# Order of the first pages, sixteen gate products moved ahead, and the chunk recurrence as a thread of its own

## The chip, the cores and the metric

The kernel runs on one core of one Trainium2 chip. The metric is the device time of one execution in microseconds; the time before is the median of three runs. Engines are named as in the profile: PE (matmul), PEld (its weight loads), DVE (vector), ACT (scalar), POOL (GpSimd) and SP, which here only issues DMAs. A name such as L707 is a line of the kernel before.

## What is computed

One layer of a hybrid backbone: two parallel head groups over one input projection, then a gated MLP with a 3x3 convolution on a grid. D_MODEL is 2048, there are 512 latent and 256 context tokens, D_FF is 5632, all in float32. The reference, cut:

```python
mx = jnp.split(s_c @ w_ada + b_ada, 6, axis=-1)            # s_c = silu(c); mc the same for the context
h_ctx = modulate(rms_norm(ctx, g_pre_mix), mc[0], mc[1])
h_lat = modulate(rms_norm(x, g_pre_mix), mx[0], mx[1])
u_lat = h_lat @ w_in                                       # 2048 columns: 1536 for pooling, 512 for the SSM
u_ctx_ssm = h_ctx @ w_in[:, POOL_WIDTH:]
for d in range(2):                                         # two directions of a diagonal complex recurrence
    lam, bb = s5_discretise(...)                           # h_t = lam * h_{t-1} + bb u_t
    hc = s5_scan(ctx_g, lam, bb, None, rev)
    hl = s5_scan(lat_g, lam, bb, h0_from(hc), rev)
    lat_dirs.append(s5_readout(hl, c_re, c_im))
# pooling: centred means over 2, 4, 8, 16 tokens minus the token, a 384x384 matmul per group
mix = concat([pool_out, gelu(y + d*u) * sigmoid(. @ w_glu)]) @ w_out
x = x + mx[2] * rms_norm(mix, g_post_mix)
z = modulate(rms_norm(x, g_pre_ffn), mx[3], mx[4]) @ w_up
f = (val * silu(gate)) @ w_down                            # val, gate: halves of the 3x3 convolution of z
x = x + mx[5] * rms_norm(f, g_post_ffn)
```

## The kernel before

Every matmul on a weight is made of three: a weight page of 128x1024 is loaded on SP's queue (`raw`, L60), rounded by ACT to `whi` (L77), and DVE forms the rest, `wlo` = raw - whi (L78). PE then multiplies high by high, high by low and low by high (L176 to L178). `raw`, `whi` and `wlo` have two buffers each, and one page is made ahead. Each engine does its instructions in the order of the program.

The kernel goes through these stages.

*First pages.* Twelve pages of x and the context come in (`x_page`, L409), ACT squares them, and PE sums the squares over partitions into `ssl` and `ssc`. Among them `ada_round` R (L436) loads a 1 MB page of the modulation weights (`adak`, three buffers) and multiplies the condition with it; round n // 3 follows every third page. A table (`at`, `pre`) hangs other work behind given rounds: `rstd_x` behind round 4, then rows and columns of the modulation (`ada_row`, `ada_cols`), the tiles of h (L472 to L493), and pieces of the first projection (`u_piece`). `discretise1` to `discretise4` compute the powers of lam on POOL, with two sines on ACT (L321, L322); the second and third are called at page 8.

*First projection.* The columns of u for the SSM, of the latent tokens (`ul`) and the context (`uc`), go round by round with the rest of the ada rounds. POOL builds matrices `mi` (`mi_build`, L557 to L559) from the powers, and PE transposes them to `mt` (`mt_half`, L577): `mi` k behind round 13 + 3k, its halves behind 17 + 3k and 18 + 3k.

*Latent projection.* Twelve blocks of two pages (`u_block`, tile `ub`) give the pooling columns; a page is 24 matmuls. After each, `bg.tick` steps background threads (`Threads`, L90): generators that emit a little work and yield its DVE cost and a lag in pages. They are asked in the order of their priorities. `front` (0) stores u to DRAM, reads it back transposed as `UT` (SP, L658), multiplies it with `mt` into `bp` (L674), does the chunk recurrence on `B` (54 pairs of a product L691 and a sum L692 on DVE), and, once all blocks are out, goes on to the SSM's output (`SN`, `R`, E by matmuls `eb`, y). `pool_block` (1) forms the windows' means (`ps`, L854) and p (L865 to L872) from a block that ACT has evicted to `up` (L839). `gemv` (3) forms the other modulation vectors: 96 products of half a row block of `ada_n` (`gv`, 512 KB, two buffers) with the condition's row, summed by DVE (L924), in the order (vector c, block n, half).

*Pooling matmuls, output projection* (`pool_group`, `wout_block`), with the SSM output and the rest of `gemv` as threads among them.

*Turn to the FFN.* `norm_pair` (L1057) adds the first sub-layer to x, normalises, and forms h for the FFN: `macc` scaled rows, transposes to `h2p`, and `hf` (L1109, ACT L1106) with the scale and shift in `acol`. Those come from the last products: `bg.finish(gv_t)` (L1089) emits all that are left. Then come the up and down projections of the FFN.

## Time and profile before

| | before |
|---|---|
| median of three runs | 2239.28 us (2239.27 to 2248.13) |
| the profiled execution | 2241.74 us, its span 2240.0 us |
| PE busy in the span | 2098.5 us (94%) |
| DVE busy | 1543.1 us (69%) |
| ACT busy | 691.3 us (31%) |
| POOL busy | 285.3 us (13%) |
| DMA moved | 313.43 MB, a mean of 140 GB/s |

The shares are means over stages with different limits; the stages are read one by one from the table of windows in the section below. "Granted clock" is TensorE's clock as a share of the full one, as the profile records it.

### The profile page before, as it was taken

What the parts mean: (1) busy time and instruction counts of PE and PEld (TensorE: products, weight loads), DVE (VectorE), ACT (ScalarE), POOL (GpSimd) and SP (SyncE); (2) the same over time, 40 slices, a digit from 0 to 9 for tenths busy, and PEclk for the clock granted to TensorE, in tenths of its full rate; (3) what the DMA queues carried; (4) which work ended last, traced back from release to release, by engine and by line L of the source; (5) the groups of instructions that cost most, each with busy time, mean ns of one, the idle gap of its engine ahead of it and who ended that gap; (6) DMA issues with size and microseconds to landing.
All of it is one profiled execution on the core that took longest, in us unless ns stands there. A gap on an engine that the chain in (4) does not pass through costs nothing.

```text
span 2240.0 us, 24576 instructions
## 1 busy us (share of the span) xinstructions
PE 2098.5 (94%) x9500; PEld 1653.2 (74%) x9500; DVE 1543.1 (69%) x2134; ACT 691.3 (31%) x977; POOL 285.3 (13%) x334
## 2 busy tenths in 40 slices
PE   6998889899992899999999999999999999999996
PEld 3577667666772888888888888888888888888885
DVE  2543887654676588867777777777767667667676
ACT  3344215553352533332222222222222222222224
POOL 7940000571023200000000000000000000000004
PEclk9899999999995999999999999999999999999998
DMA  7855125765774423333333333333322333323335
GB/s 307 319 196 188 57 79 180 223 179 170 253 252 154 177 95 97 126 132 114 111 123 113 131 124 114 111 123 113 112 88 94 94 94 94 94 94 94 94 94 188
DMA packets 92564, 313.43 MB, mean 140 GB/s; under 512 B 16288, under 2 KB 21152, under 8 KB 88352
## 3 DMA queue, kind: packets, MB, share of 16 engines
q1 hardware_dynamic: 89920, 304.99, 40.9%
q10 hardware_dynamic: 2528, 6.88, 0.9%
q8 instruction: 74, 1.21, 0.2%
q14 instruction: 42, 0.34, 0.0%
HBM read 301.38 MB, written 10.45 MB: 139 GB/s over the span
## 4 chain that ended last, share of the span: by engine, by line
PE 65%; DMA 5%; DVE 4%; ACT 2%; issue 1%; POOL 0%; DVEq 0%; ACTq 0%; SPq 0%; POOLq 0%
PE up L177 14%; PE up L176 14%; PE up L178 14%; PE dn L176 7%; PE dn L178 7%; PE dn L177 7%; DMA gv<-in_ada_n 3%; DVE scr L924 1%; DMA raw<-in_w_out 1%; DMA raw<-in_w_up 1%; DVE wlo L78 1%; ACT scr L1038 0%; PE uh L178 0%; PE uh L176 0%; PE uh L177 0%
## 5 line engine op out<-in xcount | busy, mean ns | idle before, releaser
L78 DVE TENSOR_TENSOR wlo<-raw,whi 128x1024 fp32r<-128x1024 f32 (+1 forms) x326 | 404.6, 1241 | 422.6 <-ACT whi L77 419.7
L77 ACT ACTIVATE whi<-raw 128x1024 fp32r<-128x1024 f32 (+1 forms) x326 | 340.4, 1046 | 720.6 <-PE dn L178 313.4
L1225 DVE SCALAR_TENSOR_TENSOR cv<-zp,wconv,cv 128x512 f32<-128x512 f32 x704 | 528.3, 750 | 18.8
L176 PE MATMUL up<-h,whi 128*128 128x512 f32 x1344 | 531.3, 395 | 0.0
L177 PE MATMUL up<-h,whi 128*128 128x512 f32 x1344 | 530.9, 395 | 0.0
L178 PE MATMUL up<-h,wlo 128*128 128x512 f32 x1344 | 530.6, 395 | 0.0
L177 PEld LDWEIGHTS up<-h,whi 128*128 128x128 f32 x1344 | 252.0, 187 | 61.5
L178 PEld LDWEIGHTS up<-h,wlo 128*128 128x128 f32 x1344 | 251.9, 187 | 61.6
L176 PEld LDWEIGHTS up<-h,whi 128*128 128x128 f32 x1344 | 251.9, 187 | 61.6
L176 PE MATMUL dn<-whi,g 128*128 128x512 f32 x672 | 265.6, 395 | 0.0
L178 PE MATMUL dn<-whi,g 128*128 128x512 f32 x672 | 265.6, 395 | 0.0
L177 PE MATMUL dn<-wlo,g 128*128 128x512 f32 x672 | 265.3, 395 | 0.0
L1040 POOL TENSOR_TENSOR facc<-facc,frow 128x512 f32<-128x512 f32 x11 | 15.4, 1429 | 1437.7 <-ACT scr L1038 1437.7
L924 DVE SCALAR_TENSOR_TENSOR scr<-gv,srow 128x1024 bf16<-128x1024 f32 x96 | 131.2, 1366 | 84.0 <-DMA gv<-in_ada_n 79.0
L1259 ACT ACTIVATE zp<-up 128x512 f32<-128x512 f32 x84 | 50.6, 602 | 378.3 <-PE up L178 373.6
L178 PEld LDWEIGHTS dn<-whi,g 128*128 128x128 f32 x672 | 126.0, 187 | 31.0
L176 PEld LDWEIGHTS dn<-whi,g 128*128 128x128 f32 x672 | 126.0, 188 | 30.6
L177 PEld LDWEIGHTS dn<-wlo,g 128*128 128x128 f32 x672 | 126.0, 187 | 30.5
L1273 DVE TENSOR_TENSOR facc<-facc,dn 128x512 f32<-128x512 f32 x144 | 92.1, 681 | 0.7 <-PE dn L178 0.7
L176 PE MATMUL ub<-hT,whi 128*128 128x512 f32 x192 | 80.3, 418 | 10.6 <-ACT whi L77 10.5
L178 PE MATMUL ub<-hT,wlo 128*128 128x512 f32 x192 | 79.9, 416 | 8.9 <-DVE wlo L78 8.9
L177 PE MATMUL wo<-wlo,mx 128*128 128x512 f32 x192 | 77.0, 401 | 3.9 <-DVE wlo L78 3.9
(272 smaller groups left out, 2487.6 us busy)
## 6 DMA issues: line engine op xcount, KB each, us to landing
raw<-in_w_up SPq DMA_DIRECT2D x176, 512.0 KB
gv<-in_ada_n SPq DMA_DIRECT2D x128, 512.0 KB
raw<-in_w_down SPq DMA_DIRECT2D x88, 512.0 KB
adak<-in_ada_k SPq DMA_DIRECT2D x32, 1024.0 KB
raw<-in_w_out SPq DMA_DIRECT2D x32, 512.0 KB
raw<-in_w_inp SPq DMA_DIRECT2D x24, 512.0 KB
xl<-in_xT SPq DMA_DIRECT2D x8, 512.0 KB
raw<-in_w_ssm SPq DMA_DIRECT2D x8, 512.0 KB
```

The lines of the kernel that those rows point to most:

```text
L77: nc.scalar.activation(hi[:, :n], raw[:, :n], AF.Copy)
L78: nc.vector.tensor_tensor(lo[:, :n], raw[:, :n], hi[:, :n].bitcast(F32), op=OP.subtract)
L176: PE.matmul(o, ahi, bhi, start=start, stop=False)
L177: PE.matmul(o, ahi, blo, start=False, stop=False)
L178: PE.matmul(o, alo, bhi, start=False, stop=stop)
L924: V.scalar_tensor_tensor(scr[:], tiles[x][:], 1.0, srow[:, hf * 1024:(hf + 1) * 1024], op0=OP.mult, op1=OP.mult, accum_out=gacc[:, hf, c, ...
L1040: eng.tensor_tensor(m, m, row[d // 2][:, d % 2, :], op=OP.mult)
L1225: V.scalar_tensor_tensor(a[:], zz, wcol, a[:], op0=OP.mult, op1=OP.add)
L1259: S.activation(zp[j][i % 2][:, 1:9, 1:65], o.rearrange("p (r c) -> p r c", r=8), AF.Copy)
L1273: V.tensor_tensor(f, f, os[t], op=OP.add)
```

## The change

1. *First pages.* An ada round follows every second page, six among the pages for four before. `rstd_x` hangs behind round 5, `discretise2` and `discretise3` (before at page 8) behind round 7, `discretise4` behind 8. `mi` k is built behind round 14 + 4k, its halves are transposed behind 20 + 4k and 21 + 4k.
2. *Gate products.* Eight pages of 1 MB, each both halves of one block of the first vector, are loaded behind rounds 32 to 39 into the buffers of `adak`; two products each behind rounds 35 to 42. `gemv` leaves these 16 out.
3. *Recurrence.* It is a thread `scan` of priority 2, added when the last `bp` is out: behind `pool_block`, ahead of `gemv`. `front` goes on when blocks and `scan` are done. The lags in `front` around the store, UT and `bp` are longer.

```diff
@@ the table of rounds
-        at(13 + 3 * k, lambda k=k: mis.update({k: mi_build(k, pg("mi"), ...)}))
+        at(14 + 4 * k, lambda k=k: mis.update({k: mi_build(k, pg("mi"), ...)}))
         for r in range(2):
-            at(13 + 4 + 3 * k + r, lambda k=k, r=r: mt_half(k, r))
-    at(4, rstd_x)
-    at(5, discretise4)
+            at(20 + 4 * k + r, lambda k=k, r=r: mt_half(k, r))
+    at(5, rstd_x)
+    at(7, discretise2)
+    at(7, discretise3)
+    at(8, discretise4)
+    gpair = {}
+
+    def gpair_load(nt):
+        gpair[nt] = p0.tile([128, 2, 1024], F32, name="adag", tag="adak", bufs=3)
+        nc.sync.dma_start(gpair[nt][:], A["ada_n"][0, nt].rearrange("a p n -> p a n"))
+
+    def gpair_dot(nt):
+        g = gpair.pop(nt)
+        for hf in range(2):
+            V.scalar_tensor_tensor(scr[:], g[:, hf], 1.0, srow[:, hf * 1024:(hf + 1) * 1024], op0=OP.mult,
+                                   op1=OP.mult, accum_out=gacc[:, hf, 0, nt:nt + 1])
+
+    NGP = 8
+    for nt in range(NGP):
+        at(32 + nt, lambda nt=nt: gpair_load(nt))
+        at(35 + nt, lambda nt=nt: gpair_dot(nt))
@@ the twelve pages
-        if n == 8:
-            discretise2()
-            discretise3()
-        if n % 3 == 2:
-            ada_round(n // 3)
-            for f in rounds.get(n // 3, []):
+        if n % 2 == 1:
+            ada_round(n // 2)
+            for f in rounds.get(n // 2, []):
                 f()
-    for R in range(4, max(rounds) + 1):
+    for R in range(6, max(rounds) + 1):
@@ front, and the recurrence taken out of it
+    def scan():
+        ...
+        for c0 in (0, 16):
+            yield cma(B[:, c0 + 1:c0 + 16:2], B[:, c0:c0 + 15:2], l4[:, 0], 8), 0
+        ...
     def front():
         mi_next(NMT)
-        yield 0.0, 0.4
+        yield 0.0, 1.2
         ...                                     # UT loads
-        yield 0.0, 0.4
+        yield 0.0, 1.6
         ...                                     # k >= NMT: mt_half, mi_next
-                    yield 0.0, 0.2
+                    yield 0.0, 0.4
         ...                                     # bp
-                yield 0.0, 0.2
-        for c0 in (0, 16):
-            yield cma(B[:, c0 + 1:c0 + 16:2], B[:, c0:c0 + 15:2], l4[:, 0], 8), 0
-        ...
+                yield 0.0, 1.6 if k == NMT else 0.3
+        sc_t = bg.add(scan(), 2)
 
         while not ub_done:
             yield 0.0, 1
+        while not sc_t[2]:
+            yield bg._step(sc_t), 0
@@ gemv
-        todo = [(c, n, hf) for c in range(3) for n in range(16) for hf in range(2)]
+        todo = [(c, n, hf) for c in range(3) for n in range(16) for hf in range(2)][2 * NGP:]
-            gv_state[0] = x + 1
+            gv_state[0] = 2 * NGP + x + 1
```

The order that this gives is shown at three places. In it a line of the changed kernel is about 20 higher than the same line of before (from L650 on; ahead of that it differs by 0 or 1).

ACT's queue among the last of the twelve pages, before. `sq` are the squares, `sm` the sines of discretise2, `adar` a copied row of the modulation, `rst` part of rstd_x:

```order
L420 ACTIVATE sq<-xc_301 128x1024
L321 ACTIVATE sm<-sm 128x32
L322 ACTIVATE sm<-sm 128x32
L420 ACTIVATE sq<-xl_357 128x1024
L420 ACTIVATE sq<-xl_363 128x1024
L420 ACTIVATE sq<-xc_369 128x1024
L450 ACTIVATE adar<-ada_254 128x512
L403 ACT_TABLE_LOAD
L403 ACTIVATE rst<-rv 128x512
```

And in the changed kernel:

```order
L451 ACTIVATE adar<-ada_247 128x512
L420 ACTIVATE sq<-xc_316 128x1024
L420 ACTIVATE sq<-xl_324 128x1024
L420 ACTIVATE sq<-xl_337 128x1024
L420 ACTIVATE sq<-xc_343 128x1024
L403 ACT_TABLE_LOAD
L403 ACTIVATE rst<-rv 128x512
L403 ACTIVATE rst<-rv 128x256
L451 ACTIVATE adar<-ada_329 128x512
L321 ACT_TABLE_LOAD
L321 ACTIVATE sm<-sm 128x32
```

The sines have moved behind `rst`, with a load of ACT's function table of their own, and the first copy of an ada row stands ahead of the last four squares.

DVE's queue in the latent projection, between the splits of two pages, before. `sct` and `B` are the recurrence, `ps` and `p` the pooling:

```order
L78 TENSOR_TENSOR wlo<-raw,whi 128x1024
L691 TENSOR_TENSOR sct<-B,lp_86 128x512
L692 TENSOR_TENSOR B<-B,sct 128x8x64
L691 TENSOR_TENSOR sct<-B,lp_86 128x512
L692 TENSOR_TENSOR B<-B,sct 128x8x64
L854 TENSOR_TENSOR ps_1996<-up 128x527
L854 TENSOR_TENSOR ps_1998<-ps_1996 128x525
L854 TENSOR_TENSOR ps_2000<-ps_1998 128x521
L865 SCALAR_TENSOR_TENSOR p_1904<-ps_2000,up 128x512
```

And in the changed kernel:

```order
L78 TENSOR_TENSOR wlo<-raw,whi 128x1024
L875 TENSOR_TENSOR ps_2191<-up 128x527
L875 TENSOR_TENSOR ps_2193<-ps_2191 128x525
L886 SCALAR_TENSOR_TENSOR p_2201<-ps_2193,up 128x512
L888 TENSOR_TENSOR p_2201<-ps_2193,rcnt 128x2
L889 TENSOR_TENSOR p_2201<-p_2201,up 128x2
L892 TENSOR_TENSOR p_2201<-ps_2193,rcnt 128x1
L893 TENSOR_TENSOR p_2201<-p_2201,up 128x1
L666 TENSOR_TENSOR sct<-B,lp_86 128x64
L667 TENSOR_TENSOR B<-B,sct 128x64
```

The pooling of a block now stands ahead of the recurrence. The recurrence stands in pages 7 to 18 of the 24 before, and in pages 12 to 24 and the eight pooling-matmul pages behind them now. On PE, 36 matmuls of `ub` stand ahead of the first `bp` before, and 78 now.

DVE's queue in the turn to the FFN, before. `scr,gacc<-gv,srow` is a gate product, `macc` the rows that are normalised:

```order
L1083 TENSOR_SCALAR macc_3766<-xin,st_1359 128x1024
...
L924 SCALAR_TENSOR_TENSOR scr,gacc<-gv,srow 128x1024 x3
L1037 TENSOR_TENSOR macc_3767<-macc_3767,wq_4745 128x512
L1037 TENSOR_TENSOR macc_3768<-macc_3768,wq_4746 128x512
L924 SCALAR_TENSOR_TENSOR scr,gacc<-gv,srow 128x1024 x2
L1037 TENSOR_TENSOR macc_3767<-macc_3767,wq_4786 128x512
L1040 TENSOR_TENSOR macc_3767<-macc_3767,pio 128x512
L1037 TENSOR_TENSOR macc_3768<-macc_3768,wq_4787 128x512
L1040 TENSOR_TENSOR macc_3768<-macc_3768,pio 128x512
L924 SCALAR_TENSOR_TENSOR scr,gacc<-gv,srow 128x1024 x9
L934 TENSOR_TENSOR acol<-gacc 128x16
```

And in the changed kernel:

```order
L944 SCALAR_TENSOR_TENSOR scr,gacc<-gv,srow 128x1024 x2
L1057 TENSOR_TENSOR macc_3768<-macc_3768,wq_4762 128x512
L1057 TENSOR_TENSOR macc_3769<-macc_3769,wq_4763 128x512
L944 SCALAR_TENSOR_TENSOR scr,gacc<-gv,srow 128x1024
L954 TENSOR_TENSOR acol<-gacc 128x16
L955 TENSOR_TENSOR acol<-acol,colp 128x16
L959 TENSOR_SCALAR acol<-acol 128x16
L960 TENSOR_TENSOR acol<-acol,colp 128x16
L1057 TENSOR_TENSOR macc_3768<-macc_3768,wq_4800 128x512
L1060 TENSOR_TENSOR macc_3768<-macc_3768,pio 128x512
L1057 TENSOR_TENSOR macc_3769<-macc_3769,wq_4801 128x512
L1060 TENSOR_TENSOR macc_3769<-macc_3769,pio 128x512
```

Of 14 products that stood there 3 are left, and `acol` stands ahead of the last `macc` rows.

## Rows read from the trace of the kernel before

**Rows 1.** Windows by stage: stretch, its length, busy us of each engine (instructions), granted clock.

```profile
0.00:73.00 73.00, 49.98 (x214) 23.17 (x215) 24.13 (x49) 26.49 (x37) 57.79 (x156) 0.85 0.83 324
73.00:174.50 101.50, 101.50 (x635) 71.63 (x635) 47.69 (x48) 34.44 (x53) 64.85 (x52) 0.99 0.64 236
174.50:335.60 161.10, 129.81 (x579) 103.02 (x578) 113.88 (x203) 44.52 (x86) 9.18 (x6) 0.92 0.32 102
335.60:667.00 331.40, 313.44 (x1453) 238.58 (x1451) 217.98 (x311) 149.72 (x230) 92.71 (x66) 0.99 0.65 210
667.00:716.50 49.50, 7.79 (x33) 6.21 (x33) 27.85 (x50) 9.33 (x22) 9.78 (x7) 0.56 0.57 192
716.50:2240.00 1523.50, 1495.96 (x6592) 1210.62 (x6592) 1111.55 (x1477) 426.83 (x551) 50.99 (x49) 0.99 0.34 112
```

**Rows 2.** Waits of PE from 0 to 785 us: total us, times, longest.

```profile
PE uh L176 <- ACT hf L1106: 25.5, 1, 25.5
...
PE h2p L1099 <- DVE macc L1037: 16.8, 4, 8.8
...
PE ub L176 <- ACT whi L77: 10.5, 5, 3.7
...
PE ub L178 <- DVE wlo L78: 8.9, 7, 4.0
...
PE pp L178 <- DVE wlo L78: 1.6, 2, 1.1
```

**Rows 3.** Windows of four slow stretches in the latent projection: the first, and their sum.

```profile
188.30:198.50 10.20, 5.31 (x21) 4.96 (x22) 0.00 (x0) 2.06 (x6) 0.00 (x0) 0.50 0.57 162
...
sum 27.00, PE 19.22 PEld 16.00 DVE 16.18 ACT 2.06 POOL 0.00; mean PE 4.80 PEld 4.00 DVE 4.05 ACT 0.51 POOL 0.00
```

**Rows 4.** Timeline, first pages, several engines: start, us, instruction, [idle before <-releaser].

```profile
35.98 0.23 ACT L321 ACTIVATE sm<-sm 128x32 f32<-128x32 f32 x1 [13.07 <-POOL sm L272]
...
37.33 5.40 PE L422 MATMUL ssl<-sq,ones 128*128 128x512 f32 x8 [3.61 <-ACT sq L420]
...
44.38 1.92 PE L444 MATMUL ada<-adak,scol 128*32 128x512 f32 x16
...
48.09 0.69 DVE L404 TENSOR_TENSOR rt<-rst 128x512 f32<-128x512 f32 x1 [4.55 <-ACT rst L403]
...
61.88 1.40 DVE L472 SCALAR_TENSOR_TENSOR xl<-xl,scsh,rst 128x512 f32<-128x512 f32 x2
```

**Rows 5.** Timeline of POOL: the starts of the first and the third `mi`.

```profile
77.23 1.12 POOL L557 TENSOR_TENSOR mi<-bb,pio 128x512 f32<-128x512 f32 x1
...
92.67 1.57 POOL L557 TENSOR_TENSOR mi<-bb,pio 128x512 f32<-128x512 f32 x1
```

**Rows 6.** Timeline of SP's queue and of PE around UT.

```profile
183.30 12.20 SPq L658 DMA_DIRECT2D UT<-u_scratch  x4
...
193.19 3.70 PE L674 MATMUL bp<-UT,mt 128*128 128x96 f32 x16 [10.08 <-DMA UT<-u_scratch]
```

**Rows 7.** DVE by line, 174.5 to 335.6: form, count, busy us, mean ns, idle before.

```profile
L692 DVE TENSOR_TENSOR B<-B,sct 128x512 f32<-128x512 f32 (+4 forms) x54 | 27.6, 512 | 1.9
L691 DVE TENSOR_TENSOR sct<-B,lp 128x512 f32<-128x512 f32 (+4 forms) x52 | 27.1, 520 | 1.3
```

**Rows 8.** Timeline of DVE: a gate product beside POOL's work, and one without.

```profile
431.05 2.29 DVE L924 SCALAR_TENSOR_TENSOR scr<-gv,srow 128x1024 bf16<-128x1024 f32 x1
...
678.58 1.22 DVE L924 SCALAR_TENSOR_TENSOR scr<-gv,srow 128x1024 bf16<-128x1024 f32 x1 [4.76 <-DMA gv<-in_ada_n]
```

**Rows 9.** Timeline of DVE in the turn to the FFN.

```profile
680.99 1.28 DVE L1037 TENSOR_TENSOR macc<-macc,wq 128x512 f32<-128x512 f32 x2
...
687.05 0.68 DVE L1037 TENSOR_TENSOR macc<-macc,wq 128x512 f32<-128x512 f32 x1
...
690.71 0.69 DVE L1040 TENSOR_TENSOR macc<-macc,pio 128x512 f32<-128x512 f32 x1 [0.85 <-ACT scr L1038]
...
714.98 0.54 DVE L1109 TENSOR_SCALAR hf<-h2p,acol 128x256 f32<-128x256 f32 x1
```

More of the change, by code (lines that the diff above doesn't have):

```diff
@@ L434, in emit @@
     ada = {}
+    gacc = cst("gacc", [128, 2, 4, 16])
     def ada_round(R):
@@ L591, in emit @@
     for k in range(NMT):
-        at(13 + 3 * k, lambda k=k: mis.update({k: mi_build(k, pg("mi"), tb[:].rearrange("p a b -> p (a b)"))}))
+        at(14 + 4 * k, lambda k=k: mis.update({k: mi_build(k, pg("mi"), tb[:].rearrange("p a b -> p (a b)"))}))
         for r in range(2):
-            at(13 + 4 + 3 * k + r, lambda k=k, r=r: mt_half(k, r))
-    at(4, rstd_x)
-    at(5, discretise4)
+            at(20 + 4 * k + r, lambda k=k, r=r: mt_half(k, r))
[16 more added lines that the diff above has]
+        at(35 + nt, lambda nt=nt: gpair_dot(nt))
     at(6, lambda: W.load(2))
@@ L908, in pool_evict @@
             yield 0.65, 0
-    gacc = cst("gacc", [128, 2, 4, 16])
     acol = cst("acol", [128, 4, 16])
```

74 lines of the change are left out of this document (37 added, 37 removed).

## Prediction

> **What bounds the kernel now.** I read the profile from the coarse to the fine. First the table of windows, cut by stage [rows 1]: PE is busy 1495.96 of the 1523.50 us behind 716.5, almost all of it the FFN, 313.44 of 331.40 before that, and all of 101.50 in the first projection. The time that can be had lies in three stretches: the first pages (49.98 busy of 73.00, granted clock 0.85), the latent projection from 174.5 to 335.6 (129.81 of 161.10, clock 0.92) and the turn to the FFN (7.79 of 49.50, clock 0.56). PE's waits say what is late there [rows 2]: 25.5 us for `hf` and 16.8 us for `macc` in the turn; in the projection 10.5 us for `whi`, 8.9 us for `wlo` and, from its timeline, 10.08 us for UT [rows 6]. They cost more than their own length: behind four of them the granted clock is 0.50, the lower level (1.2 GHz) [rows 3]. Then each wait is followed back in the timelines.
>
> So the kernel is PE-bound except where three things stop PE, and the change touches all three. It adds no PE work and takes none away. The question is which waits go, and which come.
>
> **First pages (0 to 73).** In ACT's queue the two `sm` activations of discretise2 stand ahead of the last three squares; ACT waits 13.07 us for POOL, till 35.98, and PE waits 3.61 us for the next square and then does eight sums in 5.40 us [rows 4], at the low clock by its window. Moving discretise2 behind rstd_x takes that wait away. PE doesn't win all of it: ahead of the end of the sums (44.38, where ada rounds follow, two in 1.92 us [rows 4]) it now has two more ada rounds and ACT's copy of an ada row, some 2 us. Without the wait the sums end 3.61 us earlier, and some 1.7 us more by the clock; with the new work about 42.5 to 43. The two rounds are done early, not added, so they come back. Then rstd no longer waits 4.55 us for ACT [rows 4], since that copy stood just there. L472, which starts the first h tile at 61.88, should come near 58 to 59. I take **-3**: the pages of rounds 7 to 11 and the first splits still stand between it and the first matmuls. Bounds: -6, the chain with nothing else in the way; and +2, if the x pages, now behind 2 MB more on SP's queue (6.5 us at the 324 GB/s of [rows 1]), outlast the slack that ACT's 13.07 us leave.
>
> **First projection (73 to 174.5).** It is all PE [rows 1], so only a loss is possible. Two edits threaten it. (a) The 16 products come here: at 1.22 us [rows 8] and a short read of the accumulator, 16 x 1.3 = 21 us on a DVE that is busy 47.69 of 101.50 [rows 1]. Eight of them stand ahead of the `wlo` of the second ub page, 10.4 us, but spread over the last four rounds; that split is due one page (5.6 us) into the next stage. Their 8 MB share the DMA with a stage that moves 236 GB/s as a mean. SP's queue holds the weight pages of ub behind them. (b) POOL starts to build the matrices `mi` some 20 us later, at about 97 for 77.23 [rows 5], because discretise2 to 4 start later. The first two took from 77.23 to 92.67 [rows 5], 3.9 us a half, so the first half stands at 101, or 105 if POOL's start is later than that; PE reaches its transpose, moved from round 17 to round 20, at about 105. PE's queue is in order: the ends are 0 and 4 us. Each later `mi` has four rounds for its 7.7 us, so nothing accumulates. I take **0**, range 0 to +4.
>
> A rule of the Trainium skill speaks against (a). What the trace shows first: a product took 2.29 us at 431.05, with POOL busy beside it, and 1.22 us alone [rows 8]. "SBUF — State Buffer", section "Who interferes with whom", says that a VectorE instruction with two SBUF inputs contends with a GpSimd instruction that reads SBUF, for a port that one holds at a time; the two rows agree. By that rule, if POOL still builds when the products come, they cost 16 x 2.3 = 37 us, the eight ahead of `wlo` 18 us, and PE would stand for some 6 us. By [rows 5] six builds from 97 on end near 143, before the products come, and I give the rule little weight.
>
> **Latent projection (174.5 to 335.6) and the pooling matmuls behind it.** It takes 161.1 us: 129.81 busy and 31.2 of waits or gaps [rows 1]. At the low clock a matmul takes twice as long, so half of the busy time in the four slow stretches, 19.22/2 = 9.6 us [rows 3], is loss too. The floor is about 120.
> - *UT.* SP issues the four loads at 183.30 and takes 12.20 us over it; PE, with `bp` queued behind 36 matmuls of ub, waits 10.08 us, from 183.1 to 193.19 [rows 6]. With the longer lags 78 matmuls stand before it: 42 more at 8.6/36 = 0.24 us are 10.0 us of cover. The wait shrinks to about 1 (0 to 4), and the low clock at 188.3 goes.
> - *Recurrence.* 27.6 + 27.1 = 55 us of DVE [rows 7] stand in pages 7 to 18, ahead of the pooling. ACT's evictions wait for the pooled pages, then the splits, then PE: the `whi` and `wlo` waits, 19.4 us, and three of the slow stretches. Adding up the durations of the rows in the program's order, DVE has 87.6 us of work in those eleven pages, splits included, against 11 x 5.6 = 61.6 us of PE: it is the bound there, by 26. In the new order pooling goes first and the recurrence fills pages 12 to 24 and the pooling-matmul pages behind. The same sum gives 76.3 us against 67.2 in twelve pages; a second `wlo` buffer absorbs some 3.4, which leaves **5.7** of waits; and 26.1 against 22.4 us in the pooling-matmul pages, **3.7**, where the trace has 1.6 [rows 2].
> - *Sum.* Gone: 31.2 + 9.6 = 40.8. Left or new: UT 1, 5.7, 2.1 net behind 335.6, and 2 to 3 of low clock behind those. **-29** (-15 if overload and clock come to twice or three times that; -36 if DVE fits).
>
> **From there to 667: 0** (+-4). The remaining products still come at about two a page. The recurrence ends some ten pages ahead of the first `eb`, which the program has half a page later, 2.8 us, on cover that stays.
>
> **Turn to the FFN (667 to 716.5).** `hf` waits for the last gate vector, and for that DVE must do all products. 14 stand there, most waiting on their loads; `hf` starts at 714.98 [rows 9]. With 16 gone earlier 3 are left. Two of them wait for loads behind the same four `xin` loads as now: the second started at 678.58 after a wait of 4.76 us [rows 8], and the third was over by 680.99 [rows 9]. Then two `macc` sums (1.28 us), 0.9 us of vector work, and the last four `macc` rows, which took from 687.05 to 691.40 = 4.35 us [rows 9]: 681 + 1.3 + 0.9 + 4.35 = 687.6, where `hf` starts. 714.98 - 687.6 = **-27** (-20 if a load comes 3 us late and more low clock follows; -33 if those four rows go at once behind 680). Late next are these `macc` rows and their transposes.
>
> **Sum.** -3 + 0 - 29 + 0 - 27 = -59. The profiled execution took 2241.74 us (1.7 more than its span), 2.5 above the median of 2239.28. 2241.7 - 59 = 2182.7, and on the median **2180**. About 0.5%, 11 us, is what a measurement of this kernel can tell from no change.
>
> **Rivals.**
> 1. *DVE remains the bound* (0.20). The 55 us don't vanish, they move; if pages with pairs still outlast PE's and the low clock follows each wait, the stage gives UT and little more, about 10 of the 29. For: 87.6 us became 76.3 + 26.1 over more pages. Against: from 335.6 to 667 DVE is busy only 217.98 of 331.40 [rows 1]. 2180 + 19 = 2199.
> 2. *Only the turn gains* (0.08): rival 1 without a gain at UT, and the first pages give nothing. 2239 - 27 = 2212.
> 3. *All covered* (0.09): no overload, no UT wait, the first pages give 6 and the turn 32. 2180 - 15 = 2165.
> 4. *Gains eaten* (0.04): the turn waits for another load as late as the last one now, and rival 1 holds; within 11 us of 2239.
> 5. *Slower* (0.03), by one mechanism: SN and the whole SSM output hang on the end of the recurrence, and `eb` stands in PE's in-order queue. If the thread behind the pooling ends so late that this chain isn't done, PE stands for it: 55 us of recurrence and some 14 of chain, less the 27 and 29 won, 2239 + 13 = 2252. It decides when the last pair comes later than about six pages ahead of `eb`; the program has ten.
>
> By the port rule of the Trainium skill the time would be 2180 + 6 = 2186, inside the forecast's own range; it has 0.1 of its chance.
>
> **How the numbers follow.** The forecast has 0.56, the rivals 0.20, 0.08, 0.09, 0.04 and 0.03. The terms' likelier ends put the forecast itself at 2168 to 2195; to leave no more than 2 in 10 out the range reaches down past rival 3 to 2158 and up through rival 1 to 2208. Faster by over 0.5%: 0.56 + 0.20 + 0.08 + 0.09 = 0.93; within 0.5% 0.04; slower 0.03.
>
> **What would show it.** `hf` should start some 27 us earlier in its stage and its wait fall from 25.5 to a few us; UT's wait fall under 4 us; the waits for `whi` and `wlo` together from 19.4 to under 10; ACT's wait of 13.07 us go. Wrong would be: a PE wait over 4 us at the first `mtp` or at the second ub page, a projection stage over 150 us, or a new wait at `eb`.

## The result: 1.1% faster, two fifths of what was forecast

The changed kernel takes 2218.17 us (median of four runs, 2216.93 to 2220.76) against 2242.66 us of the kernel before on the same chip (four runs, 2239.27 to 2248.13): a ratio of 0.989 [0.9864, 0.9916]. That is faster by more than 0.5%, but 10 us above the upper end of the forecast range, and 24 us were won where 59 were summed up. (The forecast counted from 2239.28 us, the median of three of these four runs.) The profiled execution took 2217.68 us, its span is 2215.9 us.

The windows of the changed kernel by stage, columns as in [rows 1]. The bounds differ from [rows 1], since one stage is cut into three here: 177 to 361 is all of the latent projection, 361 to 398 the pooling matmuls, 398 to 671 the output projection and what follows it.

```profile
0.00:73.00 73.00, 49.73 (x216) 24.23 (x217) 26.02 (x49) 28.53 (x39) 41.63 (x113) 0.87 0.88 335
73.00:177.00 104.00, 101.25 (x633) 70.99 (x632) 52.94 (x62) 33.44 (x52) 72.28 (x89) 0.99 0.74 273
177.00:361.00 184.00, 160.98 (x721) 129.48 (x721) 140.04 (x246) 54.93 (x101) 18.55 (x12) 0.93 0.42 138
361.00:398.00 37.00, 30.12 (x109) 22.15 (x108) 30.25 (x51) 23.83 (x36) 0.00 (x0) 0.91 0.29 91
398.00:671.00 273.00, 256.63 (x1200) 195.54 (x1199) 163.34 (x221) 114.47 (x179) 90.35 (x66) 0.97 0.63 207
671.00:697.00 26.00, 7.82 (x32) 6.28 (x32) 16.02 (x31) 11.56 (x26) 9.65 (x7) 0.59 0.53 198
697.00:2216.00 1519.00, 1493.67 (x6592) 1209.04 (x6592) 1113.97 (x1479) 426.83 (x552) 51.92 (x49) 0.99 0.34 112
```

PE's waits of the changed kernel from 0 to 800 us, total, times and longest, the lines that answer to [rows 2]:

```profile
PE ub L178 <- DVE wlo L78: 19.8, 6, 9.4
PE h2p L1119 <- DVE macc L1057: 17.3, 4, 6.7
...
PE yb L764 <- DMA Mi<-e_scratch: 6.9, 2, 4.9
PE pp L177 <- DVE ph L904: 5.1, 3, 4.1
PE rowb L1021 <- issue: 4.6, 1, 4.6
...
PE ub L176 <- ACT whi L77: 3.1, 1, 3.1
...
PE uh L176 <- ACT hf L1126: 1.1, 1, 1.1
```

The `hf` wait of 25.5 us is gone, and so is the one for UT. But the `wlo` wait of the projection grew from 8.9 to 19.8 us, with one of 9.4 us in it, the pooling matmuls have waits for `ph` that weren't there, and two behind them are longer (`yb` 6.9 us for 4.1, `rowb` 4.6 for 2.2). The windows say the same by stage: the turn is about half as long as in [rows 1], the granted clock of the projection is 0.93, as it was before over the same pages (174.5 to 369.2), and that of the output projection fell from 0.99 to 0.97.

Where the time went is best read by lining up the same PE work in both traces: the starts of the first matmul of a page, before and after.

| PE starts | before | after | difference | forecast of the stretch | measured |
|---|---|---|---|---|---|
| last piece of `ul` | 166.15 | 164.54 | -1.61 | -3 | -1.6 |
| first page of `ub` | 174.54 | 177.09 | +2.55 | 0 (0 to +4) | +4.2 |
| 8th page of `ub` | 246.01 | 258.16 | +12.15 | | +9.6 |
| 19th page of `ub` | 335.60 | 324.42 | -11.18 | | -23.3 |
| first page of `wo` | 397.28 | 397.65 | +0.37 | -29 for these three | +11.5 |
| last page of `wq` | 660.83 | 665.39 | +4.56 | 0 | +4.2 |
| first page of `uh` (FFN) | 716.49 | 697.13 | -19.36 | -27 | -23.9 |
| first page of `up` | 784.80 | 760.87 | -23.93 | | -4.6 |

The turn gave nearly what was forecast. The latent projection with its pooling matmuls gave 2.2 of 29 us: 23.3 were won in pages 8 to 18, and 9.6 lost ahead of them and 11.5 behind. The start of the 8th page isn't quite the same point of the work: ahead of it PE has done 8 transposing and 16 `bp` matmuls fewer than before, so the loss ahead of it is a little larger than 9.6, and the win behind it too. Those three pieces, the 4.2 us ahead of `ub`, and the turn are what the experiments take apart.

The last row has no term in the forecast: from the first `uh` to the first `up` page it is 63.7 us for 68.3. PE's waits for `whi` there fall from 5.0 to 0.7 us, its busy time from 59.3 to 56.9. In all kernels with at most three products left at the turn this stretch takes 63.1 to 64.2 us, and 66.6 to 69.2 in those with six or more.

### The profile page after: what moved, and what is told of

It reads as the page before. It is cut to its first block, busy times and chain, and to the rows that moved or that the text cites. A ratio compares the mean times of both kernels' runs of the same rounds, so it can differ in the third digit from the quotient of the medians.

```text
span 2215.9 us, 24553 instructions
## 1 busy us (share of the span) xinstructions
PE 2100.2 (95%) x9500; PEld 1657.7 (75%) x9500; DVE 1542.6 (70%) x2134; ACT 693.6 (31%) x978; POOL 284.4 (13%) x334
## 3 DMA queue, kind: packets, MB, share of 16 engines
q1 hardware_dynamic: 89792, 304.99, 41.1%
## 4 chain that ended last, share of the span: by engine, by line
PE 69%; DMA 4%; DVE 3%; ACT 2%; issue 2%; POOL 0%; DVEq 0%; SPq 0%; ACTq 0%; POOLq 0%
PE up L176 14%; PE up L178 14%; PE up L177 14%; PE dn L178 7%; PE dn L176 7%; PE dn L177 7%; DMA gv<-in_ada_n 2%; PE wo L176 1%; PE eb L822 1%; PE wo L177 1%; PE wo L178 1%; DMA Mi<-e_scratch 1%; DVE scr L944 1%; ACT scr L1058 1%; DMA rawb<-in_w_up 0%
## 5 line engine op out<-in xcount | busy, mean ns | idle before, releaser
L1060 POOL TENSOR_TENSOR facc<-facc,frow 128x512 f32<-128x512 f32 x11 | 15.4, 1424 | 1434.8 <-ACT scr L1058 1434.8
L944 DVE SCALAR_TENSOR_TENSOR scr<-gv,srow 128x1024 bf16<-128x1024 f32 x80 | 112.8, 1410 | 63.0 <-DMA gv<-in_ada_n 59.2
L178 PE MATMUL ub<-hT,wlo 128*128 128x512 f32 x192 | 79.6, 414 | 19.8 <-DVE wlo L78 19.8
L176 PE MATMUL wo<-whi,mx 128*128 128x512 f32 x192 | 79.4, 414 | 0.0
```

Of the source, the lines that this page charges most:

```text
L176: PE.matmul(o, ahi, bhi, start=start, stop=False)
L178: PE.matmul(o, alo, bhi, start=False, stop=stop)
L944: V.scalar_tensor_tensor(scr[:], tiles[x][:], 1.0, srow[:, hf * 1024:(hf + 1) * 1024], op0=OP.mult, op1=OP.mult, accum_out=gacc[:, hf, c, ...
L1060: eng.tensor_tensor(m, m, row[d // 2][:, d % 2, :], op=OP.mult)
```

## What the trace of the changed kernel shows at these places

**Ahead of `ub`.** The timeline of SP's queue: start, time taken to issue, what is loaded.

```profile
145.09 24.24 SPq L604 DMA_DIRECT2D adag<-in_ada_n  x4
169.38 0.46 SPq L60 DMA_DIRECT2D raw<-in_w_inp  x1
171.50 9.12 SPq L604 DMA_DIRECT2D adag<-in_ada_n  x2
180.71 0.89 SPq L60 DMA_DIRECT2D raw<-in_w_inp  x2
181.65 13.25 SPq L172 DMA_DIRECT2D gv<-in_ada_n  x4
...
195.49 16.02 SPq L700 DMA_DIRECT2D UT<-u_scratch  x4
211.57 2.79 SPq L172 DMA_DIRECT2D gv<-in_ada_n  x2
```

A 1 MB load waits for one of three buffers, and a buffer comes free when DVE has done its two products. While it waits, SP issues nothing else: four loads take 24.24 us, and the weight page of `ub` behind them goes out at 169.38. SP's own waits from 130 to 230 us name the products (L609):

```profile
SPq L604 <- DVE scr L609: 32.4, 5, 17.3
```

In ACT's timeline the first two pages of `ub` wait for it:

```profile
175.50 1.06 ACT L77 ACTIVATE whi<-raw 128x1024 fp32r<-128x1024 f32 x1 [11.57 <-DMA raw<-in_w_inp]
...
186.51 1.06 ACT L77 ACTIVATE whi<-raw 128x1024 fp32r<-128x1024 f32 x1 [8.99 <-DMA raw<-in_w_inp]
```

And in PE's timeline, the second page's wait and two further on:

```profile
187.62 0.80 PE L176 MATMUL ub<-hT,whi 128*128 128x512 f32 x1 [3.10 <-ACT whi L77]
...
203.67 0.79 PE L178 MATMUL ub<-hT,wlo 128*128 128x512 f32 x1 [6.18 <-DVE wlo L78]
...
220.91 0.80 PE L178 MATMUL ub<-hT,wlo 128*128 128x512 f32 x1 [9.42 <-DVE wlo L78]
```

The UT loads are issued from 195.49, where [rows 6] has 183.30.

**The `wlo` waits.** PE waits 6.18 and 9.42 us for a split. DVE's timeline shows why it is late:

```profile
201.24 1.23 DVE L944 SCALAR_TENSOR_TENSOR scr<-gv,srow 128x1024 bf16<-128x1024 f32 x1 [7.82 <-DMA gv<-in_ada_n]
...
202.39 1.22 DVE L78 TENSOR_TENSOR wlo<-raw,whi 128x1024 fp32r<-128x1024 f32 x1
...
218.48 1.22 DVE L944 SCALAR_TENSOR_TENSOR scr<-gv,srow 128x1024 bf16<-128x1024 f32 x1 [13.70 <-DMA gv<-in_ada_n]
...
219.63 1.22 DVE L78 TENSOR_TENSOR wlo<-raw,whi 128x1024 fp32r<-128x1024 f32 x1
```

The split isn't waiting for its own page. A gate product stands ahead of it in DVE's queue and waits 7.82 and 13.70 us for its load. The second of these loads is one that SP issues at 211.57, behind UT. The first is issued ahead of UT, at 191.40, when the product before has freed its buffer, and isn't there until 201.24. The wait has moved from `bp` to a queue that every page of `ub` runs through. The clock is at its lower level around all of this; windows of the four slow stretches (177.3 to 225.1), their sum, with as much time as in [rows 3]:

```profile
sum 27.30, PE 18.07 PEld 14.08 DVE 18.98 ACT 6.22 POOL 6.08; mean PE 4.52 PEld 3.52 DVE 4.74 ACT 1.56 POOL 1.52
```

**The pooling matmuls.** PE's timeline has the longest of the waits for `ph`:

```profile
371.93 0.79 PE L177 MATMUL pp<-ph,whi 128*128 128x512 f32 x1 [4.14 <-DVE ph L904]
```

The window of the 8 us around it, columns as in [rows 1], shows the granted clock at 0.79 and DVE busy 5.61 us:

```profile
371.00:379.00 8.00, 7.07 (x24) 5.67 (x25) 5.61 (x10) 1.54 (x2) 0.00 (x0) 0.79 0.12 37
```

**The turn.** DVE's timeline, for [rows 9]:

```profile
679.91 1.38 DVE L944 SCALAR_TENSOR_TENSOR scr<-gv,srow 128x1024 bf16<-128x1024 f32 x1 [1.36 <-ACT scr L1058]
...
685.32 1.23 DVE L944 SCALAR_TENSOR_TENSOR scr<-gv,srow 128x1024 bf16<-128x1024 f32 x1 [4.02 <-DMA gv<-in_ada_n]
686.47 1.28 DVE L1057 TENSOR_TENSOR macc<-macc,wq 128x512 f32<-128x512 f32 x2
...
688.76 1.63 DVE L944 SCALAR_TENSOR_TENSOR scr<-gv,srow 128x1024 bf16<-128x1024 f32 x1 [1.01 <-ACT scr L1058]
...
695.76 0.69 DVE L1060 TENSOR_TENSOR macc<-macc,pio 128x512 f32<-128x512 f32 x1 [0.85 <-ACT scr L1058]
696.37 0.54 DVE L1129 TENSOR_SCALAR hf<-h2p,acol 128x256 f32<-128x256 f32 x1
```

Three products are left, as the forecast had it, and they stand among the `macc` rows. From the start of the last `wq` page to the first `uh` page it is 31.7 us, for 55.7 before.

## The experiments

Every time is a median beside runs of the kernel before on the same chip, whose medians lie between 2242.66 and 2243.57 us. Each edit is against the changed kernel where nothing else is said. "Products left" are gate products that DVE hasn't begun when PE starts the last page of `wq`; "the turn" is from there to the first page of `uh`.

**One part at a time.** Two theories of the loss at the start of `ub`: SP's queue, held by the 1 MB loads (Q in the expectations); and the recurrence's thread with its longer lags (L).

Without the pairs:
```diff
-    NGP = 8
+    NGP = 0
```


> The changed kernel without its second part: all 96 gate products are in the background thread again, the order of the first pages and the recurrence thread with the longer lags stay. Theory Q (the 1 MB pages hold SP's queue, so the weight pages of the latent projection, the store of u, UT and the gate vectors behind UT all come late): the first ub matmul comes 2 to 4 us ahead of before (174.54) instead of 2.55 behind, the eleventh ub page about 10 us ahead instead of 4 behind, no wait for wlo over 4 us ahead of bp; the turn to the FFN has its 25 us wait for hf back. Time 2217.7 - 14 + 25 = about 2229. Rival L (the longer lags and the order of the thread are what delays the pages ahead of the eleventh): the first ub matmul is early, but the eleventh page is still some 4 us behind before; time about 2240.

2250.59 us, 1.0032 [1.0023, 1.0042]: no gain is left. The start is as Q has it: the first page of `ub` stands 0.4 us ahead of before for 2.6 behind, the 12th 10.4 ahead for 4.3 behind, so the pairs cost some 15 us there. But the time is that of neither theory (2229 and 2240): 19 products are left and the turn takes 73.4 us, 18 more than before.

The pairs alone (pages, products and `gemv`'s shorter list, in the kernel before):

> The kernel before with the second part of the change alone: 8 pages of 1 MB and 16 products among the first projection, 80 products in the thread. Theory Q: the first ub matmul comes 4 to 5 us behind before, UT and the pages behind it later still, so that the eleventh ub page is 10 to 15 us behind; the recurrence then slips on, and about 8 to 12 us are lost by the pooling matmuls; the turn gains 24 to 27. Time about 2239 - 15 = 2224. Rival L: the pages cost 3 to 5 us and nothing behind them; time 2216.

2216.76 us, 0.9889 [0.9872, 0.9905], as much as the whole change. The number is L's (2216), the trace isn't: the `bp` wait is longer than in [rows 6], and 17.1 us are lost by the 12th page of `ub` and 19.1 by the last `wq` page, where L has nothing behind the first 3 to 5. SP's queue in this kernel:

```profile
147.84 24.30 SPq L602 DMA_DIRECT2D adag<-in_ada_n  x4
```

PE's timeline in it, for [rows 6]:

```profile
210.68 3.70 PE L691 MATMUL bp<-UT,mt 128*128 128x96 f32 x16 [14.58 <-DMA UT<-u_scratch]
```

No product is left, and the turn falls to 16.0 us, which pays 39.7 where 24 to 27 were expected.

The recurrence's thread and the longer lags alone, in the kernel before:

> The kernel before with the third part alone: the recurrence as a thread behind the pooling and the longer lags. Theory Q: UT's wait of 10 us goes, since nothing holds SP's queue, the eleventh ub page is 8 to 12 us ahead of before, the pages behind it gain some 15 more, and the pooling matmuls give 9 to 11 back, the output projection 5 to 7. Time 2239 - 10 = 2229 (2225 to 2234). Rival L: the lags move the wait and no more; the eleventh page gains nothing, time 2238 to 2245.

2252.24 us, 1.0046 [1.0031, 1.0061], above both theories. UT's wait is gone and `wlo`'s is 18.4 us, 13.3 of it at once. DVE's timeline in this kernel:

```profile
204.97 1.22 DVE L945 SCALAR_TENSOR_TENSOR scr<-gv,srow 128x1024 bf16<-128x1024 f32 x1 [15.58 <-DMA gv<-in_ada_n]
206.12 1.22 DVE L78 TENSOR_TENSOR wlo<-raw,whi 128x1024 fp32r<-128x1024 f32 x1
```

And SP's queue:

```profile
183.92 14.26 SPq L701 DMA_DIRECT2D UT<-u_scratch  x4
198.27 2.75 SPq L172 DMA_DIRECT2D gv<-in_ada_n  x2
```

So the moved wait doesn't need the pairs: UT's loads hold SP, the gate loads behind them are late, and the split stands behind the product. PE is still 24 us ahead of before at the 18th page of `ub`, 12 at the first `wo`, and then 19 products are left for 14: the turn takes 73.0 us and gives all of it back.

The order of the first pages alone, in the kernel before:

> The kernel before with the first part alone: six ada rounds among the pages, discretise2 to 4 later, mi and its transposes four rounds apart. Both theories: the first projection's matmul starts some 4 us earlier, then waits about 4 us for the second h tile, and the first ub matmul comes 2 to 3 us ahead of before (174.54); everything behind it is moved by as much. Time 2236 to 2237. If the gain grows to 5 us or more, the lead of the first matmul is lost to something that the other parts bring; if it is zero, the lead that is seen at the first matmul is eaten by the first projection itself.

2242.23 us, 0.9999 [0.999, 1.0009]. The 5.5 us at the first matmul of `ul` are 1.0 at the first page of `ub`, and nothing that the time shows, where 2 to 3 us were expected.

**The start.** Theory Q against DVE itself (D): eight products stand ahead of the second page's split.

```diff
-        at(35 + nt, lambda nt=nt: gpair_dot(nt))
+        at(33 + nt, lambda nt=nt: gpair_dot(nt))
```


> The changed kernel with the two products of a 1 MB page two rounds earlier (behind rounds 33 to 40, loads where they were). Theory Q (a page's load waits for the buffer that an earlier product frees, and SP's queue waits with it): the buffers come free some 5 to 8 us earlier, so the first weight page of the latent projection is issued near 162 instead of 169.38, the first ub matmul comes at 173 to 175 instead of 177.09, and by the eleventh ub page 6 to 8 us are won; time 2218.2 - 7 = 2211. Rival D (the DVE time of the 16 products, 21 us, is what costs, wherever they stand): the first ub matmul stays at 176 to 178, and the time at 2216 to 2219.

2207.47 us, 0.9845 [0.983, 0.986]. Buffers come free two rounds earlier, the weight page is issued at 164.23, and the 12th page of `ub` stands 10.6 us ahead of that of the changed kernel. The time is 4 us below Q's number (2211) and 9 below D's (2216 to 2219), and the weight page goes out near Q's 162. Only the first `ub` matmul, at 176.05, is where D has it; but PE no longer waits for weights there, and the second page comes 6.0 us earlier than in the changed kernel. The two `wlo` waits behind it remain, at 6.7 and 8.5 us.

The 1 MB loads on another queue:
```diff
-        nc.sync.dma_start(gpair[nt][:], ...)
+        nc.gpsimd.dma_start(gpair[nt][:], ...)
```


> The changed kernel with the eight loads of 1 MB issued on POOL's queue instead of SP's; products and order as they are. Theory Q: SP isn't held, the three weight pages are issued by 150 to 165 as before, the first ub matmul comes near 172.5, UT's loads and the gate vectors behind them 8 to 10 us earlier, no wait for wlo over 4 us ahead of bp: 2218.2 - 12 = 2206. Rival D (the products' own DVE time): the first ub matmul near 176, time 2214 to 2218.

2211.72 us, 0.9859 [0.9844, 0.9873], between Q's number and D's. The first page of `ub` comes as in the kernel before (174.50), so the held queue was what delayed it. But then SP spends 20.69 us from 172.48 on four `gv` loads, and the `wlo` waits are 24.3 us, where Q has none over 4: the hold went to the next load in the queue that waits for a buffer (SP's waits for the `gv` products are 17.6 us there, 10.0 in the changed kernel).

**The moved wait.** If the split is late because of a product with a late load, it must be in time when `gemv` starts later (on top of the earlier products):
```diff
+        yield 0.0, 4
```


> The run with the products two rounds earlier (2207.47), with the background products starting four pages later. Theory G (in the pages ahead of bp a product stands in DVE's queue waiting for a load that SP issues behind UT, and the wlo of the next page stands behind that product): the two wlo waits of 6.7 and 8.5 us ahead of bp go or fall under 2 us each, the eleventh ub page comes 10 to 14 us earlier than in that run (272.88); 4 or 5 products fewer are done by the turn, which grows by 13 to 18 us: time 2205 to 2212. Rival W (the weight pages themselves are late behind UT, products or not): the wlo waits become whi waits of the same length, the eleventh page stays within 3 us, and the time is 2220 to 2225.

2214.09 us, 0.9863 [0.9849, 0.9878], a little above the forecast of it, but the mechanism is shown; PE's waits from 175 to 337:

```profile
PE ub L178 <- DVE wlo L78: 4.9, 6, 2.5
```

The 12th page of `ub` is 21.2 us ahead of before, 14.9 more than with the products alone. But ten products are left for three, the turn takes 48.7 us for 31.8, and nothing of it is left at the end.

UT's loads on POOL's queue, so that no `gv` load stands behind them (also on top of the earlier products):
```diff
-            nc.sync.dma_start(u, ...)       # UT
+            nc.gpsimd.dma_start(u, ...)
```


> The run with the products two rounds earlier, with UT's four loads issued on POOL's queue instead of SP's; nothing else. Theories G and W: gate vectors and weight pages are no longer behind UT, the two wlo waits of 6.7 and 8.5 us go, the eleventh ub page comes 10 to 14 us earlier than 272.88 and the number of products done stays: time 2207.5 - 11 = 2196 (2193 to 2200). Rival U (UT's packets, small ones, hold the DMA engines whatever queue issues them, so that the loads beside them are late all the same): 2204 to 2210.

2204.1 us, 0.982 [0.9805, 0.9834]: 3 us less at the medians (the intervals overlap), the long waits for `wlo` are 4.4 us each. That is the number of the rival U. UT didn't start earlier, since POOL builds a last `mi` ahead of it: the first load goes out at 188.51, where SP issued it at 187.22. Then POOL's timeline:

```profile
198.03 1.29 POOL L700 DMA_DIRECT2D UT<-u_scratch  x1 [5.53 <-DMA u_scratch<-uc]
205.93 1.29 POOL L700 DMA_DIRECT2D UT<-u_scratch  x1 [6.60 <-DMA u_scratch<-uc]
```

These two loads wait for the store of their part of u to land, and from issue to landing UT's loads take 10.3 to 15.3 us. The gate loads behind UT do go out earlier, and are late all the same: one that SP issues at 192.39 is there for DVE only at 203.54, with the DMA engines busy for 0.97 of the time between:

```profile
203.54 1.23 DVE L944 SCALAR_TENSOR_TENSOR scr<-gv,srow 128x1024 bf16<-128x1024 f32 x1 [8.86 <-DMA gv<-in_ada_n]
...
192.00:204.00 12.00, 8.01 (x24) 6.05 (x24) 3.15 (x6) 1.06 (x1) 1.79 (x2) 0.74 0.97 239
```

In the changed kernel a `gv` load takes 4.7 us as a median. So part of the lateness is the traffic itself, as U has it; whether UT's loads or the store make it isn't taken apart.

**The lags.** Those of the kernel before, with the rest of the change:
```diff
-        yield 0.0, 1.2        # the others: 1.6, 0.4, and 1.6 or 0.3
+        yield 0.0, 0.4        #             0.4, 0.2, and 0.2
```


> The changed kernel with the lags of before around the store, UT and bp. Theory Q: UT is late because the store and the loads are late, so with the short lags PE waits for it 14 us or so, as it does with the pages alone, but the recurrence starts some four pages earlier and less of it falls into the pooling-matmul pages, which give back 4 to 6 us: net 2220 to 2226. Rival L (the longer lags only put off the recurrence into the pages where DVE has no room, and cost more than UT's wait): 2208 to 2213.

2213.05 us, 0.9871 [0.9854, 0.9887], 5 us below the longer lags at the medians, though the intervals overlap, and at the upper end of L's range (2208 to 2213) where Q's begins at 2220. The wait for UT is back, 14.5 us, but no split is late behind it, and the recurrence starts earlier: the pooling matmuls, which cost 8.8 us in the changed kernel, cost 0.2. Six products are left, and the turn takes 33.8 us.

**The products that are left.** More pages moved ahead: ten (with the earlier products), and eleven with the short lags.
```diff
-    NGP = 8
+    NGP = 10
```


> As the run with the products two rounds earlier, but ten pages and twenty products, 76 in the thread. The thread gave 77 products by the last page of the output projection in the changed kernel and in both kernels without the pages, so none would be left for the turn. Theory T (each product left costs the turn its load and some 3 us, three of them with the wait for the first load 15.7 us: 31.7 us from the last wq page to uh against 16.0 with none left): turn 16 to 17 us, time 15 below that of the run with eight pages, less 2 to 4 for two more pages at the start: 2199 to 2201. Rival M (the rows of macc and their transposes set the turn's length when products are few): the turn stays at 28 to 32 us, time 2211 to 2215.

2203.5 us, 0.9822 [0.9807, 0.9837]. None is left, the turn is 22.0 us for 31.8 (16 to 17 were expected), but the start costs more (12th page of `ub` +2.8 for -6.3).
```diff
-    NGP = 8                                              # and the lags above, and
+    NGP = 11
-        at(35 + nt, lambda nt=nt: gpair_dot(nt))
+        at(33 + nt, lambda nt=nt: gpair_dot(nt))
```


> The changed kernel with the lags of before, products two rounds earlier and eleven pages with 22 products. With the old lags the thread has 74 products by the last page of the output projection, so none is left for the turn. Theory T: the turn falls from 33.8 us to 16 to 22, the earlier products bring 5 to 9 more: 2213 - 13 - 6 = 2194 (2190 to 2200). Rival M (the turn is bound by the rows of macc): 2205 to 2210.

2189.16 us, 0.9754 [0.9735, 0.9773], the best of all, 29 us below the changed kernel. Its window of the pooling matmuls, from 10 us ahead of them:

```profile
345.00:382.00 37.00, 35.16 (x148) 27.24 (x147) 30.22 (x52) 27.67 (x41) 0.00 (x0) 1.00 0.44 143
```

The pooling matmuls run at full clock, no product is left, and the turn takes 17.5 us. UT's wait is 8.2 us. Its loads on POOL's queue:

> As the run with eleven pages and the lags of before, with UT's loads on POOL's queue. With the short lags PE itself waits for UT, 14.5 us. If UT is late because SP issues it behind gate vectors and weight pages, its loads now start right behind the store and the wait falls to 8 to 10 us, the one of before: 6 to 8 us less than the run beside it, about 2187. If the transfer itself is what takes that long, the two runs are alike within 3 us.

2195.61 us, 0.9778 [0.9755, 0.9801]: no gain, the wait for UT is 11.7 us. POOL's timeline:

```profile
198.64 5.39 POOL L700 DMA_DIRECT2D UT<-u_scratch  x4
```

POOL's queue has the last `mi` build ahead of these loads, so they go out at 198.64, where SP issued the first at 191.50 in the kernel beside it. They don't wait for the store here. The first is there for PE 7.7 us later (10.2 on SP's queue), the four land 7.6 to 15.4 us after their issue. So this run doesn't free UT from a queue, it puts it into another; what it does show is that the transfer alone takes most of the wait.

Pairs alone with the earlier products, in the kernel before, without the thread, the longer lags and the first pages' order:

> The kernel before with the pages of 1 MB alone, products behind rounds 33 to 40: neither the order of the first pages nor the recurrence thread. The pages alone with late products gave 2216.76 with the turn at its shortest (16.0 us, no product left). Theory Q: earlier products win 6 to 9 us at the start here too: 2208 to 2211. Then the recurrence thread, which alone cost 9.5 us, would be worth 20 us once the products fit (2189.16 with eleven pages and the short lags). Rival: the start costs the same here, 2216, and the thread's worth is up to 27 us.

2205.78 us, 0.9831 [0.9815, 0.9846]. The start costs 5.6 to 7.2 us for 17 in the pairs alone, and the turn is 15.2 us, with nothing left. The 16.6 us to the best version are what the thread (with short lags) and the first pages are worth once no product is left, three more pages included.

Twelve pages, loaded as soon as a buffer is free, `gemv` three pages later, the long lags:
```diff
+    dot_at = [33, 34, 35, 36, 37, 37, 38, 39, 39, 40, 41, 42]
...
+        yield 0.0, 3
```


> The changed kernel with three cures at once: twelve pages whose products stand behind rounds 33 to 42, closer together, each load right behind the product that frees its buffer; the background products starting three pages later. Theory G and T together: no wlo wait behind UT, 22 to 25 us ahead of before at the output projection as with the later background products (25.1), and a turn of 16 to 22 us: 2243 - 22 - 35 = 2186 (2180 to 2190). Rival (twelve pages cost what the later products win: ten of their products stand ahead of the second split of the latent projection, 13 us of DVE against a page of 5.6): 2192 to 2198.

2192.39 us, 0.9765 [0.9745, 0.9785], the rival's number: ten products now stand ahead of the second page's split, that page's weights are late with them (PE waits 6.90 us for `whi`), it comes 14.4 us behind that of before, and the pooling matmuls lose 8.2 us again. Is that the recurrence that starts late by the lags? With shorter lags between the `bp` groups alone:
```diff
-                    yield 0.0, 0.4
+                    yield 0.0, 0.2
...
-                yield 0.0, 1.6 if k == NMT else 0.3
+                yield 0.0, 0.8 if k == NMT else 0.2
```


> As the run beside it, with the lags between bp groups shortened (0.2, and 0.8 ahead of the last two) while the lags ahead of UT and bp stay long. Theory P (the recurrence that spills into the pooling-matmul pages costs 10 to 12 us there, since DVE also splits ph and the weights): it ends about two pages earlier, and the loss from the first pooling matmul to the output projection falls from about 7 to 11 us to under 3: 3 to 8 us less than the run beside it, unless some products more are left for the turn (one to three: +5 to +15). Rival: the loss stays, and the time is the same or higher.

2200.52 us, 0.9806 [0.9791, 0.9821]. The loss in the pooling matmuls is gone (-13.5 at the first of them, -13.8 at the first `wo`), as that reason has it, though half of it is lost in the pages ahead instead (with the long lags it is -17.8 at the first pooling matmul). The time isn't better: three products are left again and the turn takes 30.4 us for 20.2.

**All runs by what is left.** Products left at the last `wq` page, and the turn:

| left | the turn, us (kernels) |
|---|---|
| 0 | 15.2 to 22.0 (pairs alone, pairs with early products, ten pages, eleven pages twice, twelve pages) |
| 3 | 30.4 to 32.5 (changed kernel, early products, both other queues, twelve with shorter lags) |
| 6 | 33.8 (lags of before) |
| 10 | 48.7 (`gemv` later) |
| 14 | 52.5 and 55.7 (first pages alone, before) |
| 19 | 73.0 and 73.4 (thread alone, without pairs) |

The number left orders the turn in all fifteen experiments, before and after, wherever the PE work ahead of it stood.

## Why the forecast was wrong, step by step

**The turn: right.** -23.9 for -27, by the mechanism named: three products stand between `macc` rows, and these rows and their transposes are late next. What the forecast didn't see is that the last three still cost 10 to 16 us: with ten pages for eight the turn falls from 31.8 to 22.0 us, and the pairs alone, with none left, have 16.0. One of the three waits 4.02 us for its load, and the `macc` rows stand behind it at the low clock (0.59 in the window of the turn).

**First pages: right in the wait, wrong in what is next.** ACT's 13.07 us for POOL are gone, and 10.69 us for PE's ada round came in their place, ahead of the copy that the change put there (ACT's timeline of the changed kernel):

```profile
34.54 0.60 ACT L451 ACTIVATE adar<-ada 128x512 f32<-128x512 f32 x1 [10.69 <-PE ada L445]
```

In PE's timeline the round behind the last sums, and the second tile of h:

```profile
44.41 1.06 PE L445 MATMUL ada<-adak,scol 128*32 128x512 f32 x8
...
71.34 0.80 PE L177 MATMUL ul<-hT,whi 128*128 128x512 f32 x1 [3.91 <-DVE hT L481]
```

The round behind the sums starts at 44.41, where it started at 44.38 in [rows 4]: nothing is won there, where the forecast had the sums end at 42.5 to 43 (its own terms, 3.61 and 1.7 less and some 2 more, come to 41.1). The h tile starts at 58.24 all the same, in the forecast 58 to 59, by another way: its modulation row, which DVE had waited for till 61.80, is there earlier. The first `ul` matmul comes 4.3 us earlier and its second tile of h doesn't: 3.91 us of wait take the lead back. The first-pages run says the same without the other parts.

**First projection: named and priced at nothing.** "SP's queue holds the weight pages of ub behind them" stands in the forecast, with no term. It measured +4.2 us at the first page of `ub`, 4.9 more by the second, and in the pairs alone 17 by the 12th. The step that was missing: a load into a buffer that isn't free holds the whole queue until it is, so its price is what stands behind it, here the weight pages, UT and the gate loads. POOL's late `mi` cost nothing: no wait for the first `mtp` remains.

The port rule of the Trainium skill didn't come to bear, as the forecast had it: POOL had done its building (its builds end at 149.6, the first product starts at 160.29), and all 16 products took 1.22 to 1.23 us. Two `gv` products beside POOL's last build took 2.13 and 2.01 us, which agrees with "SBUF — State Buffer", "Who interferes with whom"; DVE's timeline, one of each:

```profile
177.73 1.22 DVE L609 SCALAR_TENSOR_TENSOR scr<-adag,srow 128x1024 bf16<-128x1024 f32 x1
...
189.24 2.13 DVE L944 SCALAR_TENSOR_TENSOR scr<-gv,srow 128x1024 bf16<-128x1024 f32 x1
```

**UT: the step that failed most.** The forecast took 10.08 us of wait to about 1, and the low clock with it, and put nothing in its place. The `bp` wait did go. But the later UT loads stand in SP's queue ahead of gate loads, the products that wait for these stand in DVE's queue ahead of the splits, and PE waits there: 9 us of wait and 2.7 of low clock (half of 5.31 in [rows 3]) were to be won, and the first seven pages lost 9.6, with as much low clock in them alone (half of 18.07) as the whole projection had before. The late `gemv` shows it (no wait over 2.5 us is left), the thread alone shows that the pairs aren't needed for it. Not all of it is the place behind UT: the first of the two late loads goes out ahead of UT, and on POOL's queue the waits were shorter but not gone. How much of the 9.6 is the late start of SP's queue, how much the gate loads' place and how much their slow landing isn't split exactly: the earlier products took 10.6 us off the 12th page, the late `gemv` 14.9 more.

**Recurrence: right in the pages, wrong behind them.** From the 8th to the 19th page 23.3 us were won; in pages 12 to 24 there are 3.7 us of waits for `wlo`, where 5.7 were forecast. But 8.8 us were lost from the first pooling matmul to the first `wo`, where 2.1 and 2 to 3 of clock were, since the longer lags start the recurrence later and DVE then has it beside `ph`. Short lags take the loss to 0.2, and in the twelve pages' pair of runs it goes with them alone.

**Behind the projection: the term 0 was wrong twice.** The thread stands ahead of `gemv`, so by the last `wq` page the changed kernel's background has done 77 products where before had 82. That isn't seen on PE there; it is paid in the turn, and the thread alone pays so much that it ends slower than before. The forecast had the stream at "about two a page" throughout and never counted it against the recurrence that it puts in front. The other 4.2 us are later: with the same 1178 matmuls, from the first `wo` to the last `wq` page PE is busy 251.4 us for 248.0, at a granted clock of 0.97 for 0.99: three slow stretches, around the waits for `yb` (two) and `rowb`, where before had two. The waits of this stretch add up to about the same (16.3 us for 15.6). Why the stretches come is argued from the timeline alone, no run was made for it, and it stays open.

Of the forecast's own signs, `hf`, UT and ACT's wait went as it said, none of its signs of being wrong came, and one failed: the waits for `whi` and `wlo` together are 22.9 us where under 10 were to be left.

So of the rivals it was closest to "only the turn gains" in time, though not in the way: the latent projection gained, and gave it back at both its ends. The best version (2189.16) sits 9 us above the forecast, inside its range, with products done earlier, short lags and eleven pages.

## What to carry to other kernels

A load that waits for a buffer costs what stands behind it in its queue, and a compute instruction that waits for a load costs what stands behind it on its engine: before moving one, list both queues to their next time-critical entry. Work done in the background of another engine's stage has its price where its remainder must be finished; count how much of it is left at that place, since a gain that puts something ahead of it comes back there as a loss. Parts of a change that share such a stream don't add up: here the thread lost 9.5 us alone, and together with the first pages' order and three more pages of products it was worth 16.6.

## What was not expected of the hardware

Reading u back transposed takes long by itself, whatever queue issues the loads: on POOL's queue they took 10.3 to 15.3 us from issue to landing in one kernel and 7.6 to 15.4 in the other, and in the first of these kernels two of them had also waited 5.53 and 6.60 us for their part of the store. The move to that queue brought 3 us at most in one kernel and none in the other, where POOL's own work stood ahead of the loads. A gate load beside this traffic took 11 us to reach DVE, for a median of 4.7. And a queue held by a load that waits for its buffer stays held when the load is moved away, if the next load in it waits too: with the 24.24 us of 1 MB loads gone from SP, four `gv` loads held it for 20.69 us, for 13.25 before the move.
